# A diffusion trunk on one core: the instruction scheduler takes its times from another source

## Chip, core and metric

The kernel runs on one core of a Trainium2 chip. The metric is device time in microseconds (us). The median of three runs of the kernel before is 2285.17 us (2284.51 to 2285.52).

## What is computed

A trunk of two layers over 256 latent tokens and 256 context tokens of width 1024, all in float32. Each layer is a half-step SwiGLU feed-forward, three token mixers side by side (windowed attention, dense attention, a bidirectional mLSTM) with one output projection, and a second half-step feed-forward. Every one of these has a normalisation modulated by the conditioning vector (adaLN) ahead of it and a gated residual behind it. From the reference:

```
def modulated_norm(x, mod, k, norm_g):
    return rms_norm(x, norm_g[2 * k]) * (1 + mod[:, :, 3 * k + 1]) + mod[:, :, 3 * k]

def gated_residual(x, y, mod, k, norm_g, weight):
    return x + weight * mod[:, :, 3 * k + 2] * rms_norm(y, norm_g[2 * k + 1])

def half_ffn(x, mod, k, norm_g, w):
    h = modulated_norm(x, mod, k, norm_g)
    return gated_residual(x, swiglu(h, *w), mod, k, norm_g, FFN_RESIDUAL)
```

The output is the latent stream, so the last layer's output projection and last feed-forward work on the 256 latent tokens alone.

## The kernel before

Every float32 product is made of three matmuls over a high and a low half of each operand (`mm3`, L189 to L191):

```
mm(out, lh, rh, start=start, stop=False, **kw)
mm(out, lh, rl, start=False, stop=False, **kw)
mm(out, ll, rh, start=False, stop=stop, **kw)
```

Weights come in units of up to 128 x 1024. `dma_unit` (L148) loads a unit into one of 4 raw buffers by SP's queue; `cvt_unit` makes its high half on ScalarE (L158, tiles hi) and its low half on VectorE (L159, tiles lo), with 5 buffers of each. Activations are split in the same way by `split` (L184 on ScalarE, L185 on VectorE). The adaLN weights of the first sub-layer come in eight slices and are multiplied on TensorE (L315); those of later ones are multiplied on VectorE (L350, L352).

Ahead of a sub-layer each stream of 256 tokens is squared and summed (L440, ScalarE), brought to a reciprocal root by small steps on VectorE (L206 to L215), scaled (L445 VectorE, L447 ScalarE, one block of 128 tokens each), transposed on TensorE by 16 matmuls against the identity (L462), and taken out of PSUM with the modulation (L470 VectorE, L472 ScalarE). Behind it the closing matmuls of each 512 columns are summed (L490), squared (L555 ScalarE), multiplied by the gate (L557), summed up (L564) and added to the residual (L568, all VectorE). Latent and context streams follow each other, so that the matmuls of one cover the normalisation of the other.

Attention goes by items of a head and a block of queries: scores (L1005 to L1008), maximum (L1009, VectorE), exponential (L1023, ScalarE), scaling (L1035, GpSimd), transposes of the probabilities (L1047, TensorE) with a split, products with the values (L1062, L1064). Between items stand matmul groups of other projections as fillers.

`run_tasks` walks a list of tasks, each with the weight units that it needs, and writes conversions up to 2 units and loads up to 3 units ahead of the use. What it writes is not the final order: the Tile framework orders the instructions of each engine by a simulated list schedule over the whole program, in which an instruction's place comes from its dependences, its priority (the order of writing, less 400 for a few marked `URGENT`) and the times that the scheduler has for it. Engines then run their queues in that order. The context manager that does this is opened in `kernel`:

## Time and profile before

| | |
|---|---|
| median of 3 runs | 2285.17 us |
| the profiled execution | 2287.55 us |
| its span | 2285.8 us (1.75 us lie around it) |
| granted TensorE clock, mean | 0.987 |
| TensorE busy | 2203.2 us, 96% |
| VectorE busy | 1546.8 us, 68% |
| ScalarE busy | 984.7 us, 43% |
| GpSimd busy | 132.3 us, 6% |

The page is of one execution. Busy time of TensorE is the time in which a matmul is shown in flight. "Idle before" in a row, in square brackets, is the time in which the engine did nothing ahead of that instruction, with what ended it. [...]

### The profile page before, as it was taken

Reading aid. Unit: us, or ns where it says so; the run is one execution under the profiler, and the core shown is the slowest. Engines: PE = TensorE matmul, PEld = TensorE weight load, DVE = VectorE, ACT = ScalarE, POOL = GpSimd, SP = SyncE. Lnnn points to the kernel's source line nnn. Section 1 sums busy time; section 2 is a strip of 40 time slices with the busy share of each in tenths; the row PEclk is TensorE's granted clock in tenths of the full one; section 3 lists DMA queues with packets and bytes.
Section 4 is the critical chain, followed back from the end, with each engine's and each line's share of the span. In section 5 each row is a group of like instructions: output and inputs, shape, how many; then the busy total and the mean of one; then the engine's idle time right before and its main releaser. Section 6 shows DMA issues by size and latency. Waiting matters only on the chain.

```text
span 2285.8 us, 30617 instructions
## 1 busy us (share of the span) xinstructions
PE 2203.2 (96%) x11666; PEld 1843.7 (81%) x11666; DVE 1546.8 (68%) x2756; ACT 984.7 (43%) x1565; POOL 132.3 (6%) x100
## 2 busy tenths in 40 slices
PE   6999999998899999999999999999999989998998
PEld 4877777787678888888878788777778778997997
DVE  3987785788776654564444378778859877866556
ACT  3322223556677423442222253222226468755444
POOL 0000000023520000000000000000000241000000
PEclk9999999999999999999999999999999999998999
DMA  7665564421022223434434336665634203465554
GB/s 280 217 199 187 163 202 134 140 75 39 31 85 72 82 93 129 138 121 129 130 110 138 101 107 203 194 193 177 222 114 158 83 20 121 140 222 174 188 190 153
DMA packets 123523, 322.98 MB, mean 141 GB/s; under 512 B 12392, under 2 KB 25768, under 8 KB 122608
## 3 DMA queue, kind: packets, MB, share of 16 engines
q1 hardware_dynamic: 110224, 309.83, 41.9%
q10 hardware_dynamic: 13152, 11.21, 1.6%
q8 instruction: 91, 1.49, 0.3%
q14 instruction: 56, 0.46, 0.1%
HBM read 316.72 MB, written 4.28 MB: 140 GB/s over the span
## 4 chain that ended last, share of the span: by engine, by line
PE 86%; DVE 7%; ACT 4%; issue 1%; DMA 1%; POOL 1%; ACTq 0%; POOLq 0%; DVEq 0%
PE ps L189 27%; PE ps L190 27%; PE ps L191 26%; PE ps L1236 1%; DVE sm L1009 1%; ACT t L1023 1%; PE ps L1047 1%; PE ps L1205 1%; PE ps L360 1%; DVE lo L159 1%; PE ps L462 1%; POOL t L1035 1%; DVE slot L952 1%; ACT hi L158 1%; DVE t L185 1%
## 5 line engine op out<-in xcount | busy, mean ns | idle before, releaser
L158 ACT ACTIVATE hi<-raw 128x1024 fp32r<-128x1024 f32 (+1 forms) x444 | 457.0, 1032 | 785.8 <-PE ps L190 274.2
L189 PE MATMUL ps<-slot,hi 128*128 128x512 f32 (+1 forms) x2232 | 778.9, 351 | 6.0 <-ACT slot L184 5.2
L190 PE MATMUL ps<-slot,hi 128*128 128x512 f32 (+1 forms) x2232 | 776.2, 348 | 0.9 <-DVE slot L185 0.7
L191 PE MATMUL ps<-slot,lo 128*128 128x512 f32 (+1 forms) x2232 | 773.9, 347 | 0.0
L159 DVE TENSOR_TENSOR lo<-raw,hi 128x1024 fp32r<-128x1024 f32 (+1 forms) x444 | 525.9, 1187 | 286.8 <-ACT hi L158 285.1
L189 PEld LDWEIGHTS ps<-slot,hi 128*128 128x128 f32 x2232 | 420.1, 189 | 74.6 <-ACT slot L184 6.6
L191 PEld LDWEIGHTS ps<-slot,lo 128*128 128x128 f32 x2232 | 421.6, 189 | 57.9
L190 PEld LDWEIGHTS ps<-slot,hi 128*128 128x128 f32 x2232 | 421.8, 189 | 56.5 <-DVE slot L185 1.7
L189 PE MATMUL ps<-hi,slot 128*128 128x512 f32 (+2 forms) x1048 | 400.6, 383 | 2.3 <-ACT slot L184 1.1
L191 PE MATMUL ps<-hi,slot 128*128 128x512 f32 (+2 forms) x1048 | 398.6, 381 | 0.0
L190 PE MATMUL ps<-lo,slot 128*128 128x512 f32 (+2 forms) x1048 | 398.6, 380 | 0.0
L352 DVE SCALAR_TENSOR_TENSOR t<-raw,sc,t 128x1024 f32<-128x1024 f32 x224 | 280.2, 1280 | 130.7 <-DMA raw<-in_w_ada_dram 130.6
L1035 POOL TENSOR_SCALAR t<-t,sm 128x512 f32<-128x512 f32 (+1 forms) x96 | 132.1, 1388 | 1772.2 <-DVE sm L1032 1697.9
L189 PEld LDWEIGHTS ps<-hi,slot 128*128 128x128 f32 x1048 | 197.0, 188 | 46.7 <-issue 6.6
L191 PEld LDWEIGHTS ps<-hi,slot 128*128 128x128 f32 x1048 | 196.8, 188 | 39.7
L190 PEld LDWEIGHTS ps<-lo,slot 128*128 128x128 f32 x1048 | 197.0, 188 | 38.2
L184 ACT ACTIVATE slot<-t 128x512 fp32r<-128x512 f32 (+1 forms) x138 | 80.7, 594 | 188.1 <-DVE t L600 162.9
L600 DVE TENSOR_TENSOR t<-ps,t 128x512 f32<-128x512 f32 (+1 forms) x88 | 54.6, 620 | 86.5 <-PE ps L191 85.2
L185 DVE TENSOR_TENSOR slot<-t,slot 128x512 fp32r<-128x512 f32 (+1 forms) x138 | 87.4, 642 | 4.9 <-ACT slot L184 4.5
L1047 PE MATMUL ps<-ident,t 128*128 128x128 f32 x320 | 50.4, 289 | 24.2 <-POOL t L1035 16.4
L1047 PEld LDWEIGHTS ps<-ident,t 128*128 128x128 f32 x320 | 38.1, 146 | 35.4 <-POOL t L1035 23.0
L184 ACT ACTIVATE t<-ps 128x512 fp32r<-128x512 f32 x80 | 45.2, 596 | 48.9 <-PE ps L1047 44.9
(192 smaller groups left out, 1703.8 us busy)
## 6 DMA issues: line engine op xcount, KB each, us to landing
raw<-in_w_gu_dram SPq DMA_DIRECT2D x176, 512.0 KB
raw<-in_w_ada_dram SPq DMA_DIRECT2D x128, 512.0 KB
raw<-in_w_down_dram SPq DMA_DIRECT2D x92, 512.0 KB
raw<-in_w_fm_dram SPq DMA_DIRECT2D x64, 512.0 KB
raw<-in_w_br_dram SPq DMA_DIRECT2D x24, 512.0 KB
raw<-in_w_out_dram SPq DMA_DIRECT2D x24, 512.0 KB
slot<-in_w_ada_dram SPq DMA_DIRECT2D x16, 512.0 KB
raw<-in_w_down_dram SPq DMA_DIRECT2D x20, 256.0 KB
```

Of the source, the lines that this page charges most:

```text
L158: self.nc.scalar.activation(out=hi, in_=raw, func=AF.Copy)
L159: self.nc.vector.tensor_tensor(out=lo, in0=raw, in1=hi.bitcast(F32), op=ALU.subtract)
L184: self.nc.scalar.activation(out=hi, in_=src, func=AF.Copy)
L185: self.nc.vector.tensor_tensor(out=lo, in0=src, in1=hi.bitcast(F32), op=ALU.subtract)
L189: mm(out, lh, rh, start=start, stop=False, **kw)
L190: mm(out, lh, rl, start=False, stop=False, **kw)
L191: mm(out, ll, rh, start=False, stop=stop, **kw)
L352: v.scalar_tensor_tensor(out=acc, in0=units[0], scalar=c, in1=acc, op0=ALU.mult, op1=ALU.add)
L360: nc.tensor.matmul(ps[r:r + 32, :], self.ones.to_broadcast([P, 32]), st["acc"][s][:, j * 512:(j + 1) * 512], start=True, stop=True)
L600: nc.vector.tensor_tensor(out=hid[:, :W], in0=ps[:, :W], in1=hid[:, :W], op=ALU.mult)
L1035: nc.gpsimd.tensor_scalar(out=t[:, :nkey], in0=t[:, :nkey], scalar1=r[:, e:e + 1], scalar2=None, op0=ALU.mult)
L1047: nc.tensor.transpose(pt[:, n * P:(n + 1) * P], e[n % 2][:, kb * P:(kb + 1) * P], self.ident)
```

## The change

One argument of the context manager. The times by which the scheduler simulates the program come from a simulator of engine timelines instead of the framework's usual estimate. No task, tile size or operation is touched.

```
-    with tile.TileContext(nc) as tc:
+    with tile.TileContext(nc, schedule_with_timeline_sim=True) as tc:
```

TensorE, VectorE and GpSimd run the same instructions on the same tiles as before; GpSimd in the same order, SP's queue apart from its first 29 rows too. On TensorE some 2,250 instructions stand elsewhere, on VectorE 1,700, on ScalarE 800. ScalarE has 40 loads of an activation table instead of 49.

At the start, ScalarE's queue before, from the evacuation of the first adaLN products on (hi_26 to hi_51 are halves of weight units, slot_2 is the context, slot_38 the split latent tokens):

```order
L196 ACTIVATE t5_29_166<-ps_13_111 128x512
L158 ACTIVATE hi_26_156<-raw_12_109 128x1024
L472 ACTIVATE t5_43_199<-ps_42_194,modT_5_90,Amod_6_91 128x256
L158 ACTIVATE hi_31_179<-raw_22_139 128x1024
L472 ACTIVATE t5_45_209<-ps_44_204,modT_5_90,Amod_6_91 128x256
L158 ACTIVATE hi_47_227<-raw_25_149 128x1024
L184 ACTIVATE slot_38_190<-t5_43_199 128x2x256
L184 ACTIVATE slot_38_190<-t5_45_209 128x2x256
L440 ACTIVATE t5_56_268,sm_55_267<-slot_2_80 128x1024
L158 ACTIVATE hi_51_247<-raw_28_160 128x1024
```

The same place of ScalarE's queue now:

```order
L196 ACTIVATE t5_29_166<-ps_13_111 128x512
L158 ACTIVATE hi_47_227<-raw_25_149 128x1024
L440 ACTIVATE t5_56_268,sm_55_267<-slot_2_80 128x1024
L440 ACTIVATE t5_57_270,sm_55_267<-slot_2_80 128x1024
L472 ACTIVATE t5_43_199<-ps_42_194,modT_5_90,Amod_6_91 128x256
L472 ACTIVATE t5_45_209<-ps_44_204,modT_5_90,Amod_6_91 128x256
L158 ACTIVATE hi_51_247<-raw_28_160 128x1024
L184 ACTIVATE slot_38_190<-t5_43_199 128x2x256
L184 ACTIVATE slot_38_190<-t5_45_209 128x2x256
```

The two splits moved behind both squares of the context and behind hi_51; the conversions hi_26 and hi_31 moved ahead of this piece. On SP's queue three weight units, raw_11, raw_12 and raw_22, now stand ahead of the eight adaLN slices, where one did.

From the first feed-forward to the mixer in layer 0, ScalarE's queue before (slot_1 is the latent stream, ps_503 to ps_509 its transposes, hi_539 to hi_543 the halves of the units of the closing matmuls and of the mixer):

```order
L158 ACTIVATE hi_511_3168<-raw_490_3072 128x1024
L158 ACTIVATE hi_539_3260<-raw_495_3092 128x1024
L447 ACTIVATE t10_482_3013<-slot_1_79,sm_479_2998 128x1024
L472 ACTIVATE t5_504_3121<-ps_503_3116,modT_5_90,Amod_6_91 128x256
L472 ACTIVATE t5_506_3131<-ps_505_3126,modT_5_90,Amod_6_91 128x256
L184 ACTIVATE slot_499_3112<-t5_504_3121 128x2x256
```

And now:

```order
L158 ACTIVATE hi_511_3168<-raw_490_3072 128x1024
L158 ACTIVATE hi_539_3260<-raw_495_3092 128x1024
L158 ACTIVATE hi_541_3264<-raw_498_3110 128x1024
L447 ACTIVATE t10_482_3013<-slot_1_79,sm_479_2998 128x1024
L158 ACTIVATE hi_543_3268<-raw_513_3172 128x544
L555 ACTIVATE t5_514_3182,pss_485_3061<-slot_185_1229 128x512
L555 ACTIVATE t5_515_3184,pss_485_3061<-slot_185_1229 128x512
L472 ACTIVATE t5_504_3121<-ps_503_3116,modT_5_90,Amod_6_91 128x256
```

A conversion, hi_541, moved ahead of L447, and a second one with the two squares of the closing ahead of the evacuations; on TensorE the 16 transposes moved behind the last 12 closing matmuls. The other three entries of a two-stream sub-layer read alike, with one or two conversions ahead of L447.

From the mixer to the last feed-forward in layer 1, VectorE's queue before (slot_3000 is the latent stream, ps_3041 and ps_3047 the last closing sums, pss_3042 their squares):

```order
L557 TENSOR_TENSOR slot_3016_17558<-ps_3047_17677,slot_2999_17502 128x512
L211 SCALAR_TENSOR_TENSOR sm_3039_17631<-sm_3038_17630,sm_3037_17629 128x1
L564 TENSOR_TENSOR sm_3055_17717<-pss_3042_17667 128x1
L159 TENSOR_TENSOR lo_3090_17835<-raw_3053_17706,hi_3089_17834 128x1024
L215 SCALAR_TENSOR_TENSOR sm_3038_17630<-sm_3039_17631,sm_3038_17630 128x1
L206 TENSOR_SCALAR sm_3056_17719<-sm_3055_17717 128x1
L159 TENSOR_TENSOR lo_3094_17869<-raw_3081_17799,hi_3093_17868 128x1024
```

And now:

```order
L159 TENSOR_TENSOR lo_3090_17835<-raw_3053_17706,hi_3089_17834 128x1024
L568 SCALAR_TENSOR_TENSOR slot_3000_17504<-slot_3016_17558,sm_3033_17615,slot_3000_17504 128x1024
L159 TENSOR_TENSOR lo_3094_17869<-raw_3081_17799,hi_3093_17868 128x1024
L206 TENSOR_SCALAR sm_3037_17629<-sm_3035_17626 128x1
L207 TENSOR_SCALAR sm_3038_17630<-sm_3037_17629 128x1
L211 SCALAR_TENSOR_TENSOR sm_3039_17631<-sm_3038_17630,sm_3037_17629 128x1
L557 TENSOR_TENSOR slot_3016_17558<-ps_3041_17642,slot_2999_17502 128x512
L215 SCALAR_TENSOR_TENSOR sm_3038_17630<-sm_3039_17631,sm_3038_17630 128x1
L557 TENSOR_TENSOR slot_3016_17558<-ps_3047_17677,slot_2999_17502 128x512
L564 TENSOR_TENSOR sm_3055_17717<-pss_3042_17667 128x1
```

Both low halves, and the first block's L568, moved ahead of the last two L557; on ScalarE the four conversions hi_3077 to hi_3093 moved ahead of the last L440 and both L555 in the same way.

In the two attentions the filler matmuls moved ahead among the items: in layer 0 the query projections of the dense attention (four groups) and later the mLSTM's, in layer 1 one set. On VectorE some low halves and the logarithms of the mLSTM gates (L1099 to L1110) moved ahead of the key and query columns. In the very last stage three closing groups of matmuls are interleaved.

## Rows read from the trace of the kernel before

**Rows 1.** Busy us, share of the span and instructions of each engine.

```profile
PE 2203.2 (96%) x11666; PEld 1843.7 (81%) x11666; DVE 1546.8 (68%) x2756; ACT 984.7 (43%) x1565; POOL 132.3 (6%) x100
```

**Rows 2.** The chain that ended last, by engine.

```profile
PE 86%; DVE 7%; ACT 4%; issue 1%; DMA 1%; POOL 1%; ACTq 0%; POOLq 0%; DVEq 0%
```

**Rows 3.** Stretch, us; busy PE, PEld, DVE, ACT, POOL; clock; DMA share; GB/s.

```profile
0.00:57.00 57.00, 39.20 (x229) 24.45 (x229) 22.00 (x73) 21.07 (x32) 0.19 (x4) 0.94 0.77 281
...
457.00:690.00 233.00, 209.77 (x1187) 175.35 (x1186) 186.18 (x473) 150.74 (x316) 81.16 (x64) 0.96 0.18 58
690.00:1314.00 624.00, 623.38 (x2932) 514.12 (x2931) 320.32 (x603) 227.93 (x326) 0.00 (x0) 1.00 0.35 113
...
1786.00:1930.00 144.00, 127.87 (x765) 109.10 (x764) 111.46 (x252) 95.19 (x181) 50.97 (x32) 0.94 0.20 63
...
2057.00:2115.00 58.00, 47.29 (x297) 42.64 (x296) 39.98 (x75) 31.10 (x47) 0.00 (x0) 0.88 0.53 174
...
2257.00:2286.00 29.00, 19.75 (x86) 15.62 (x84) 19.59 (x38) 10.72 (x17) 0.00 (x0) 0.91 0.32 110
```

**Rows 4.** Timeline of TensorE at the start: start, duration, instruction, idle before.

```profile
27.42 0.62 PE L189 MATMUL ps<-slot,hi 128*128 128x256 f32 x3 [4.27 <-ACT slot L184]
28.76 0.58 PE L190 MATMUL ps<-slot,hi 128*128 128x256 f32 x1 [0.72 <-DVE slot L185]
...
52.82 0.66 PE L391 MATMUL ps<-ident,t 128*128 128x128 f32 x4 [0.81 <-DVE t L198]
```

**Rows 5.** Timeline of ScalarE at the start.

```profile
23.57 0.56 ACT L472 ACTIVATE t<-ps,modT,Amod 128x256 f32<-128x256 f32 x1 [0.50 <-DVE t L470]
...
26.75 1.14 ACT L184 ACTIVATE slot<-t 128x512 fp32r<-128x512 f32 x2
28.25 1.06 ACT L440 ACTIVATE t<-slot 128x1024 bf16<-128x1024 f32 x1 [0.36 <-DMA slot<-in_ctx_dram]
29.21 0.19 ACT L440 ACTIVATION_READ_ACCUMULATOR t<-slot 128x1 f32 x1
```

**Rows 6.** Timeline of ScalarE where the mixer of layer 0 is entered.

```profile
412.58 1.06 ACT L158 ACTIVATE hi<-raw 128x1024 fp32r<-128x1024 f32 x1 [0.51 <-ACT t L555]
415.38 1.06 ACT L158 ACTIVATE hi<-raw 128x1024 fp32r<-128x1024 f32 x1 [1.74 <-PE ps L191]
416.35 1.13 ACT L447 ACTIVATE t<-slot,sm 128x1024 f32<-128x1024 f32 x1
```

**Rows 7.** Timeline of TensorE at the second stream of the four entries.

```profile
435.59 1.94 PE L462 MATMUL ps<-ident,t 128*128 128x128 f32 x16 [1.57 <-DVE t L445]
...
990.61 0.66 PE L462 MATMUL ps<-ident,t 128*128 128x128 f32 x4 [0.24 <-ACT t L472]
...
1364.46 1.81 PE L462 MATMUL ps<-ident,t 128*128 128x128 f32 x12 [0.34 <-DVE t L445]
...
1756.25 0.63 PE L462 MATMUL ps<-ident,t 128*128 128x128 f32 x4 [1.25 <-DVE t L445]
```

**Rows 8.** Timeline of VectorE and TensorE from mixer to feed-forward in layer 1.

```profile
2077.40 1.23 DVE L159 TENSOR_TENSOR lo<-raw,hi 128x1024 fp32r<-128x1024 f32 x1 [0.48 <-ACT hi L158]
...
2081.07 1.12 PE L462 MATMUL ps<-ident,t 128*128 128x128 f32 x4 [5.85 <-DVE t L445]
2082.01 1.28 DVE L568 SCALAR_TENSOR_TENSOR slot<-slot,sm,slot 128x1024 f32<-128x1024 f32 x1
...
2087.04 2.82 PE L462 MATMUL ps<-ident,t 128*128 128x128 f32 x12 [4.86 <-DVE t L445]
```

**Rows 9.** TensorE's waits, 457 to 690: us in total, times, longest.

```profile
PE ps L1047 <- POOL t L1035: 10.7, 12, 2.3
PE ps L1062 <- DVE t L185: 6.1, 3, 4.5
```

**Rows 10.** Two short stretches, columns as in rows 3: the granted clock.

```profile
434.00:440.00 6.00, 3.33 (x23) 2.77 (x23) 4.25 (x11) 4.57 (x9) 0.00 (x0) 1.00 0.11 44
581.00:591.00 10.00, 7.91 (x26) 6.33 (x27) 4.21 (x9) 4.42 (x9) 3.46 (x3) 0.50 0.12 41
```

## Prediction

> **What bounds the kernel now.** I read the busy times first, then the chain that ended last, then TensorE's busy time stage by stage, and only then single waits. TensorE is busy 2203.2 of 2285.8 us [rows 1] and its matmuls are 86% of the chain [rows 2], so a new order of the same instructions can gain at most the 82.6 us in which it is idle, and little of that is free. The stages show where it lies [rows 3]: 17.8 us in the first 57, 23.2 in the layer-0 attention (457 to 690), 16.1 in the layer-1 attention (1786 to 1930), 10.7 where layer 1 goes from mixer to last feed-forward (2057 to 2115), 9.3 at the end. In the 624 us from 690 to 1314 it is idle 0.6 us. Two thirds of the kernel is therefore full, and can only lose. In the two attentions VectorE is the next engine, 186 of 233 us and 111 of 144, so idle time there isn't simply a matter of order either.
>
> The changed build holds the same tiles and tasks on TensorE, VectorE and GpSimd. ScalarE has nine fewer table loads (16 to 11 at L1218, 16 to 12 at L1312, 5 to 4 at L1023, one more at L1103). They stand almost only in the mLSTM and merge stages, inside the stretch without idle time, so I cost them at nothing: TensorE's own matmuls hide them there.
>
> **The start.** Before, TensorE's first matmul of a feed-forward comes at 27.42, after a wait of 4.27 for the split on ScalarE [rows 4]. In the new order the two splits stand behind both squares of the context stream (L440), two evacuations (L472) and the conversion hi_51. The context arrives for ScalarE at 28.25 [rows 5]. It can't come sooner: in both orders twelve 512-KB transfers are ahead of it on SP's queue, and the DMA engines carry 281 GB/s over this stage [rows 3]. So: 28.25, two L440 of 1.06 with their reads of 0.19 to 30.75, two L472 of 0.56 to 31.9, hi_51 of 1.06 to 32.9 and a first split of about 0.6 [rows 5, 6], which is 33.5 and 6 us later than before. The other move is that three weight units now pass the eight slices of the first adaLN weights on SP's queue; the last slice becomes the eleventh transfer rather than the ninth, about 3 us later. The first evacuation then moves from 23.57 to about 26.5, still ahead of 30.75, so this one is hidden by the wait for the context. What comes back: all five units are converted when the matmuls start, and the three small waits at the stage's end, of which the largest is 0.81 [rows 4], can vanish, 1.6 us together. I take **+5**; the bounds are +3 (the 0.72 at 28.76 goes as well and the smaller steps overlap) and +9 (VectorE, which now also has two adaLN products put early, gives the low half late).
>
> **Four entries with two streams** (about 416, 960, 1345 and 1728). Before, the latent stream's normalised tokens are transposed (16 matmuls, L462) among the last closing matmuls of the sub-layer that ends, so that the first matmul of the next one follows without a wait. In the new order all 16 stand behind the closing matmuls, and ScalarE has a conversion (hi_541 at the first) ahead of the normalisation L447 which feeds them. That conversion waits for a buffer which TensorE must give back: the two conversions before it start at 412.58 and 415.38, the second after a wait for TensorE [rows 6], so one buffer comes free each 2.8 us, the next at 418.2. The conversion then ends at 419.2, and L447, at 416.35 before, starts there: 2.85 us late, and with it the transposes, the evacuations behind them and the next sub-layer's first matmul. TensorE has only the closing matmuls meanwhile, which it had before too, so the 2.8 appear as a wait. Queued behind the waiting ScalarE are L447 and, on VectorE, the L470 evacuations; TensorE waits for those. A part comes back at the second stream, whose chain sets a wait of its own: 1.57 us at 435.59, 0.24 and a like piece at 991 (0.6 together), 0.34 and two like it at 1364 to 1368 (0.9), 1.25 at 1756 [rows 7]. A late TensorE finds these ready. Four times 2.8 less 4.3 is **+6.9**. Bounds: 0 if the buffers come free one unit sooner, since the closing matmuls now run without transposes between them; +11 if nothing comes back.
>
> **Mixer to feed-forward in layer 1** (2060 to 2090). One stream is left, so nothing covers the chain of the last normalisation: TensorE waits 5.85 and 4.86 us. Before, ScalarE squares the two closing halves between the conversions, and VectorE's residual step for the last block (L568) starts at 2082.01 with two low-half conversions, 1.23 us each, in its chain [rows 8]. Now four conversions on ScalarE come ahead of the squares, and both low halves and the first block's L568 ahead of VectorE's L557. The last conversion ended at 2078.6 before (2077.58 + 1.06); issued a unit earlier it ends at about 2077.4. Behind it L440 and two L555 take 2.3 us, L557 and the eight small steps 3.7 to 4.5, so the last L568 starts at 2083.4 to 2084.2 rather than 2082.01. The first block's transposes are late too, but wait for nothing else. **+2.5**, bounds 0 and +5.
>
> **The two attentions.** The projections that fill TensorE's gaps while softmax waits (23 us of query projections and 45 us of mLSTM projections in layer 0, 17 us in layer 1, by the count of their matmuls at the traced step) are moved ahead by up to 8, 12 and 11 us of work and run out sooner, at the first probability transposes rather than item by item. The waits there are mostly for GpSimd's scaling (10.7 us in 12 waits) and for VectorE's low halves (6.1 us in 3) [rows 9]. If each gap that loses its filler becomes a wait, this costs 31 us; but TensorE is not the only limit, and work done ahead shortens the gaps later, as the 4.54 at 520.42 stands just where layer 0 runs out of its first set. At best half of the 39 us now idle comes back, a gain of 20. Between these ends I choose **+4.5** for both: nearest to the sum of those gaps of 0.5 to 2.3 us which are at present covered two or three times by a filler, less the big one.
>
> **The end.** The last sub-layer's closing groups are interleaved rather than one after the other; the last 21 matmuls and the chain behind are as before. **+0.5** (0 to +1.5).
>
> Sum: 5 + 6.9 + 2.5 + 4.5 + 0.5 = **+19.4 us** on the profiled execution's 2287.55, so 2306.9; that run is 2.4 above the median of the three, so **2304.5**.
>
> **The rivals.**
> *Clock.* [...] Chance 0.14.
>
> *Packing in the attentions outweighs all else.* There the low halves, the key and query columns and the gate logarithms get new places on VectorE. If TensorE's fillers being early lets scores and transposes of the following items be issued as soon as VectorE and GpSimd are free, half of the 39 us comes back. Against the 14.9 us of the other terms that gives -5, and with the entries at their lower bound -12: 2273 to 2280. It decides if more than 19 us come back. For it speaks that waits for GpSimd dominate and GpSimd is busy only 81 of 233 us [rows 3]; against it, its order is unchanged and VectorE is 80% busy. Chance 0.13.
>
> *Nothing measurable.* The entries are absorbed (buffers come free sooner, 0), the attentions give 5 back, and start and 2080 s cost +5: 2281 to 2289. Chance 0.13, also for a build whose moves all fall into waits that stay.
>
> *All covers lost.* Start, entries and 2080 as forecast and the full 31 us in the attentions: 2330. Chance 0.06.
>
> **How the numbers follow.** My forecast, 2290 to 2315, has 0.54. The range takes in the clock rival and stops above the faster one: 2282 to 2322; about 0.13 lies below and 0.07 above. 0.2% is 4.6 us, about what a measurement of this kernel tells from no change. Slower: 0.54 + 0.14 + 0.06 = 0.74; same 0.13; faster 0.13.
>
> **What would show it.** First feed-forward matmul at 33 rather than 27.4. Before the first matmul after each of the four entries a wait of 2 to 3 us, and a smaller one for the second stream. L447 at the first entry about 2.8 us after its conversion's neighbour. The second wait around 2087 grown by 2 to 3. Idle time in the attentions within 5 us of 23 and 16. If 690 to 1314 shows idle time beyond the entry at 960, I have missed a stage; if the attentions' idle time falls by 19, the second rival is right; if the granted clock falls at the entries, the first.

## The result and the profile after

The changed kernel takes 2355.56 us (median of 4 runs, 2353.65 to 2357.57) against 2285.35 for the kernel before beside it: a ratio of 1.0306, interval 1.0294 to 1.0319. That is 70 us slower, where 19 were forecast. The profiled execution took 2356.38 us, its span is 2354.6, its mean granted clock 0.976.

From the page after: TensorE's and its neighbours' busy time, which answers to [rows 1], the chain's shares by engine, which answer to [rows 2], and the group of the first of the three products (line, engine, shapes, count; busy us, mean ns; idle before).

```profile
PE 2225.7 (95%) x11666; PEld 1864.1 (79%) x11666; DVE 1551.1 (66%) x2756; ACT 971.1 (41%) x1556; POOL 130.8 (6%) x100
...
PE 85%; DVE 7%; ACT 3%; DMA 3%; issue 2%; POOL 0%; ACTq 0%; DVEq 0%; POOLq 0%
...
L189 PE MATMUL ps<-slot,hi 128*128 128x512 f32 (+1 forms) x2232 | 779.2, 352 | 11.7 <-ACT slot L184 11.5
```

The same 11666 matmuls are busy 22.5 us longer, and the idle time is 128.9 us (2354.6 less 2225.7) where it was 82.6: 46.3 more. The two make up the span's 68.8. The longer busy time is put down to the clock: all but 1.0 us of it lies in stretches whose granted clock is lower than before, 10.9 us of it in the layer-0 attention, at 0.93 against 0.96.

To place them, each stretch of before was matched with the stretch after in which the same matmuls run (to within two of them). TensorE's windows after: stretch, us, busy (matmuls), clock, DMA share, GB/s.

```profile
0.00:104.79 104.79, 82.03 (x470) 0.95 0.70 247
...
274.68:331.13 56.45, 52.70 (x222) 0.94 0.61 183
...
411.02:477.17 66.15, 60.51 (x311) 0.95 0.38 121
477.17:742.64 265.47, 227.67 (x1220) 0.93 0.18 56
742.64:992.70 250.06, 250.06 (x1160) 1.00 0.30 100
...
1056.78:1377.36 320.58, 320.58 (x1397) 1.00 0.40 124
1377.36:1433.44 56.08, 50.11 (x333) 0.97 0.28 86
...
1765.77:1821.30 55.53, 51.85 (x269) 1.00 0.48 153
1821.30:2000.75 179.45, 156.14 (x962) 0.93 0.22 71
...
2106.90:2179.00 72.10, 58.65 (x381) 0.88 0.58 192
```

The same stretches of before lasted 100, 50, 60, 240, 250, 320, 50, 53, 170 and 70 us. The first entry, the first attention, the last entry and the second attention before:

```profile
400.00:460.00 60.00, 57.33 (x311) 1.00 0.41 133
460.00:700.00 240.00, 216.77 (x1220) 0.96 0.19 62
...
1712.00:1765.00 53.00, 51.75 (x267) 1.00 0.50 157
1765.00:1935.00 170.00, 153.87 (x964) 0.95 0.22 70
```

The differences, in us:

| stage | forecast | measured | of it busy (clock) | of it idle |
|---|---|---|---|---|
| start | +5 | +4.8 | -0.1 | +4.9 |
| before 331 (adaLN of the next sub-layer) | 0 | +6.5 | +2.7 | +3.8 |
| four two-stream entries | +6.9 | +18.8 | +6.8 | +12.1 |
| two attentions | +4.5 | +34.9 | +13.2 | +21.8 |
| mixer to feed-forward, layer 1 | +2.5 | +2.1 | -0.6 | +2.7 |
| the end | +0.5 | -0.2 | | |
| all else | 0 | +1.9 | | |

Three terms came out within 0.7 us. The entries cost nearly three times, the attentions nearly eight times their term, and one stage was not in the sum.

### The profile page after: what moved, and what is told of

Read it like the earlier page. It is cut to its first block, busy times and chain, and to the rows that moved or that the text cites. A ratio compares the mean times of both kernels' runs of the same rounds, so it can differ in the third digit from the quotient of the medians.

```text
span 2354.6 us, 30663 instructions
## 1 busy us (share of the span) xinstructions
PE 2225.7 (95%) x11666; PEld 1864.1 (79%) x11666; DVE 1551.1 (66%) x2756; ACT 971.1 (41%) x1556; POOL 130.8 (6%) x100
## 4 chain that ended last, share of the span: by engine, by line
PE 85%; DVE 7%; ACT 3%; DMA 3%; issue 2%; POOL 0%; ACTq 0%; DVEq 0%; POOLq 0%
PE ps L189 26%; PE ps L190 26%; PE ps L191 26%; PE ps L1236 1%; DMA raw<-in_w_ada_dram 1%; DVE lo L159 1%; DVE sm L1009 1%; ACT t L1023 1%; DVE t L185 1%; DVE t L352 1%; PE ps L1205 1%; PE ps L360 1%; PE ps L1047 1%; DMA slot<-in_w_ada_dram 1%; PE ps L1062 1%
## 5 line engine op out<-in xcount | busy, mean ns | idle before, releaser
L189 PE MATMUL ps<-slot,hi 128*128 128x512 f32 (+1 forms) x2232 | 779.2, 352 | 11.7 <-ACT slot L184 11.5
L191 PE MATMUL ps<-slot,lo 128*128 128x512 f32 (+1 forms) x2232 | 777.8, 349 | 0.0
L159 DVE TENSOR_TENSOR lo<-raw,hi 128x1024 fp32r<-128x1024 f32 (+1 forms) x444 | 527.8, 1190 | 311.5 <-ACT hi L158 308.3
L189 PEld LDWEIGHTS ps<-slot,hi 128*128 128x128 f32 x2232 | 422.8, 191 | 79.6 <-ACT slot L184 15.0
L191 PEld LDWEIGHTS ps<-slot,lo 128*128 128x128 f32 x2232 | 425.0, 190 | 57.3
L189 PE MATMUL ps<-hi,slot 128*128 128x512 f32 (+2 forms) x1048 | 401.6, 384 | 7.8 <-ACT slot L184 7.8
L191 PE MATMUL ps<-hi,slot 128*128 128x512 f32 (+2 forms) x1048 | 397.8, 382 | 0.0
L352 DVE SCALAR_TENSOR_TENSOR t<-raw,sc,t 128x1024 f32<-128x1024 f32 x224 | 278.9, 1281 | 153.9 <-DMA raw<-in_w_ada_dram 153.6
L189 PEld LDWEIGHTS ps<-hi,slot 128*128 128x128 f32 x1048 | 198.7, 190 | 53.2 <-ACT slot L184 8.5
L191 PEld LDWEIGHTS ps<-hi,slot 128*128 128x128 f32 x1048 | 198.2, 190 | 40.0
L1062 PE MATMUL ps<-t,slot 128*128 128x256 f32 x160 | 48.7, 323 | 22.4 <-DVE t L185 10.9
L1009 DVE TENSOR_REDUCE sm<-ps 128x1 f32<-128x512 f32 (+1 forms) x96 | 53.5, 591 | 14.0 <-PE ps L1008 13.7
```

The source lines that it names most:

```text
L159: self.nc.vector.tensor_tensor(out=lo, in0=raw, in1=hi.bitcast(F32), op=ALU.subtract)
L352: v.scalar_tensor_tensor(out=acc, in0=units[0], scalar=c, in1=acc, op0=ALU.mult, op1=ALU.add)
L1009: v.tensor_reduce(out=mx[:, e:e + 1], in_=ps[:, :nkey], axis=AX.X, op=ALU.max)
L1062: nc.tensor.matmul(o, V, hi[:, kb].rearrange("p h q -> p (h q)"), start=(kb == 0), stop=(kb == nkb - 1), skip_group_check=True)
```

## The experiments

**How they are made.** A kernel that keeps part of the old order builds the program twice, reads each engine's order from both, and builds it again with every queue tied to a chosen order by added dependences:

```
+    for stream in pin(traced):
+        for p, q in zip(stream, stream[1:]):
+            tc.add_manual_dep(traced[q], traced[p].name, mybir.DependencyInfo(
+                mybir.DependencyClass.NoSync, mybir.DependencyReason.DATA), reason="pin")
```

`KEEP` gives stretches of a queue that keep the old order, `MOVES` single instructions put behind another. All compute the whole trunk. Ratios are to the kernel before beside each run; over the study its medians were 2285.4 to 2289.0.

| run | us | ratio, interval |
|---|---|---|
| e1_l447_first | 2356.42 | 1.0313, 1.0297 to 1.0328 |
| e2_ada_behind | 2350.21 | 1.0283, 1.0266 to 1.0300 |
| e3_keys_first | 2349.60 | 1.0282, 1.0267 to 1.0297 |
| e4_attn_vec_old | 2373.70 | 1.0385, 1.0369 to 1.0400 |
| f0_new_order | 2352.43 | 1.0287, 1.0271 to 1.0303 |
| f1_attn_first_third | 2340.03 | 1.0237, 1.0217 to 1.0257 |
| f2_attn_second_third | 2339.98 | 1.0236, 1.0218 to 1.0255 |
| f3_attn_last_third | 2351.04 | 1.0283, 1.0266 to 1.0299 |
| g1_entries_old | 2334.52 | 1.0199, 1.0184 to 1.0215 |
| g2_entries_vec_old | 2367.36 | 1.0342, 1.0325 to 1.0359 |
| g3_attn1_old | 2336.94 | 1.0212, 1.0198 to 1.0226 |
| g4_old_gate_rows_later | 2289.96 | 1.0004, 0.9996 to 1.0013 |
| h1_entry_pattern_new | 2305.58 | 1.0075, 1.0058 to 1.0091 |
| h2_entry_products_old | 2359.20 | 1.0314, 1.0298 to 1.0330 |
| h3_two_vec_moves | 2288.84 | 1.0008, 0.9999 to 1.0017 |
| i1_old_order_new_deal | 2294.26 | 1.0031, 1.0019 to 1.0042 |
| i2_new_order_old_deal | 2348.88 | 1.0267, 1.0250 to 1.0283 |
| i3_two_vec_moves_old_deal | 2281.30 | 0.9974, 0.9965 to 0.9983 |

### My reason for the entries

```
+    MOVES = {'Activation': [([2642], 2450), ([8979], 8807), ([11468], 11263)]}
```

At three entries the conversion that the new order has ahead of L447 goes behind it.

> The new order, with one move on ScalarE's queue at three of the four entries (first feed-forward to mixer and second to first feed-forward in both layers; the fourth, at 960, keeps the new order): the conversion that stands ahead of the normalisation L447 is put right behind it. These three cost 14.8 us of the 70 (6.2, 6.1 and 2.5, by the traces of before and after). Theory of the prediction, that L447 waits behind the conversion and everything follows from that: most of it comes back, 2341 to 2346 us. Rival, that the evacuations of the transposes (L470, L472) stand behind the closing sums and behind further conversions anyway, so that an early L447 only waits further on: at most 3 us come back, 2352 to 2356 us.

The rival held: no gain. Two rows of ScalarE's timeline after show the conversion and L447 (start, us, instruction, idle before).

```profile
429.15 1.06 ACT L158 ACTIVATE hi<-raw 128x1024 fp32r<-128x1024 f32 x1 [1.71 <-PE ps L191]
430.12 1.13 ACT L447 ACTIVATE t<-slot,sm 128x1024 f32<-128x1024 f32 x1
```

With 11.02 us of delay by then, L447 stands at 419.1 of before's time, 2.75 later than before [rows 6], close to the forecast's 2.85. In e1 the conversion is out of the way:

```profile
422.56 1.23 DVE L159 TENSOR_TENSOR lo<-raw,hi 128x1024 fp32r<-128x1024 f32 x1 [1.05 <-ACT hi L158]
...
424.67 1.15 ACT L447 ACTIVATE t<-slot,sm 128x1024 f32<-128x1024 f32 x1 [2.15 <-DVE sm L215]
...
431.80 0.79 PE L189 MATMUL ps<-hi,slot 128*128 128x512 f32 x1 [3.54 <-ACT slot L184]
```

L447 now waits 2.15 for VectorE's L215, and TensorE's wait before its first product is 3.54 where it was 2.88. The conversion had stood in a wait that was there anyway. Ahead of that L215 VectorE has a low half (L159), which itself waits 1.05 for its high half; that this is what makes L215 late is read from the rows and not tested by a run.

### A wait that is not the order's

```
+    MOVES = {'DVE': [([1847, 1848], 1692)]}
```

Two adaLN products (L352) near 290 us go behind the four closing sums L490 that TensorE waits for.

> The new order, with one move on VectorE's queue near 290 us: the two adaLN products of one weight unit (L352), which wait for that unit's transfer, are put behind the four closing sums (L490) which free TensorE's PSUM. Theory, that an instruction waiting for a transfer holds up ready ones behind it: the 6.45 us which this stretch lost (3.75 of waiting and 2.7 at half the clock behind it) come back, 2348 to 2350 us. Rival, that the transfer itself is late and TensorE would wait for its weights instead: 0 to 2 us, 2353 to 2356 us.

It came out at 2350.2, but in the traces of e1, e3 and e4, which don't touch this place, 0.80 us of the wait was left at most. So the changed kernel was run again, as it is:

> The changed kernel as it is, beside the runs of the same call. Theory A, that the wait of 3.75 us at L360 near 298 us hangs on when two weight transfers land and not on the order alone: it is small here as in three of the four runs before, and the time is 2349 to 2352. Theory B, that the two square steps L352 ahead of four closing steps cost 6 us in every run: 2355 to 2357, as measured first, and the 6 us of the kernel with these two moved behind were its edit's.

Theory A held, at the upper edge of its range: 2352.4. VectorE and TensorE in the profile after, then in f0:

```profile
295.56 2.48 DVE L352 SCALAR_TENSOR_TENSOR t<-raw,sc,t 128x1024 f32<-128x1024 f32 x2 [2.65 <-DMA raw<-in_w_ada_dram]
...
298.69 1.94 PE L360 MATMUL ps<-t,ones 128*32 128x512 f32 x8 [3.75 <-DVE slot L490]
```

```profile
291.53 2.48 DVE L352 SCALAR_TENSOR_TENSOR t<-raw,sc,t 128x1024 f32<-128x1024 f32 x2 [2.27 <-DMA raw<-in_w_ada_dram]
...
295.18 1.06 PE L360 MATMUL ps<-t,ones 128*32 128x512 f32 x8
```

In f0 the second weight unit landed 4 us sooner and L360 ran without a wait. Of the 14 traces of a new order here, two have the long wait (3.75, and 3.99 in i2), the others 1.41 at most. It takes the new order, which has L490 behind a product that waits for a transfer, and a transfer that lands late; e2's edit was not what gained in its run. The comparisons below are with f0.

### The layer-0 attention

Four runs on what of the new order costs there, e3 and e4 first:

```
+    MOVES = {'DVE': [([3222, 3023, 3032, 3033, 3041, 3050, 3051], 2954), ([3397, 3169, 3170,
...
+                      3191], 3075)], 'Activation': [([11436, 3171], 3106)]}   # e3: behind the key and query steps
+    KEEP = {'DVE': [(449, 943)], 'Activation': [(245, 507)]}                  # e4
```

> The new order, with moves on VectorE's queue where the layer-0 attention begins: the low half lo_657 and the evacuations of the values go behind the rotation of the keys (L741), and the low half lo_703 and the logarithms of the mLSTM gates (L1099 to L1118) go behind the key and query columns (L779, L821); on ScalarE the logarithm L1103 with its table load goes behind the query columns. TensorE's fillers stay early. The layer-0 attention cost 25.5 us of the 70. Theory that VectorE's order is the cause: 8 to 20 us come back, 2335 to 2348 us. Theory of the prediction, that TensorE's fillers being moved ahead is the cause: at most 3 us come back, 2352 to 2356 us, since the scores still stand behind the fillers.

> The new order, but between 460 and 700 us of the kernel before VectorE and ScalarE keep the order of the kernel before; TensorE keeps the new one, fillers ahead. Theory that VectorE's and ScalarE's order is the cause of the 25.5 us: 20 to 25 come back, 2331 to 2336 us. Theory that TensorE's fillers ahead are the cause: 0 to 8 come back, 2348 to 2356 us. In between, both have a share and this is its size.

e3 lies between its two ranges, and e4 above both of its own. In e3 the waits at the key transposes (L815), 2.06 and 2.44 us after, became one of 0.46, and behind them the run had gained 5.6 us on the changed kernel's profile; 40 us later all but half a microsecond of that was gone. It went right behind the last products of the query projection, in waits at the probability transposes and the next scores and in slower products behind them (0.79 us for the score product L1005 below, 0.45 on the mean before):

```profile
512.15 0.30 PE L1047 MATMUL ps<-ident,t 128*128 128x128 f32 x1 [1.45 <-issue]
...
515.45 0.79 PE L1005 MATMUL ps<-slot,slot 128*128 128x512 f32 x1 [1.69 <-ACT t L1023]
```

In e4 VectorE and ScalarE run the old order and TensorE the new: 0.0098 of the time, 22 us, over f0, and the stretch is 21 us longer in its trace. So beside TensorE's new order the new vector orders save time; what they would cost beside its old order isn't shown. Then the whole order, third by third:

```
+    KEEP = {'PE': [(2047, 2360)], 'DVE': [(449, 602)], 'Activation': [(245, 304)], 'SP': [(166, 189)]}   # f1
+    KEEP = {'PE': [(2360, 2660)], 'DVE': [(602, 746)], 'Activation': [(304, 374)]}                       # f2
+    KEEP = {'PE': [(2660, 3266)], 'DVE': [(746, 952)], 'Activation': [(374, 516)]}                       # f3
```

> New order, but in the first third of the layer-0 attention (460 to 522 us of before, key and query steps and the first score products) TensorE, VectorE, ScalarE and SyncE keep the order of before. Theory local: a stretch loses by its own order; the lag of the changed kernel grows there from 17.1 to 26.5 us, so this gains 9, with 2340 to 2348. Theory passed on: as with the key steps put first (5.6 us gained by 500 us, gone by 540), what is gained is waited for in the next third, and this gains under 3.

> New order, but in the second third of the layer-0 attention (522 to 576 us of before: score products of the middle heads, value transposes, gate of the memory branch) all engines keep the order of before. Theory local: the lag grows there from 26.5 to 40, so this gains 13, with 2335 to 2344. Theory passed on: the gain is under 4, as the first third has already delayed VectorE and what it feeds.

> New order, but in the last third of the layer-0 attention (576 to 709 us of before) all engines keep the order of before. Theory local: the lag moves there from 40 to 42.6 us (with 47 between), so this gains 3, with 2347 to 2354. Theory passed on: most of the 25 us of this attention is only paid here, where fewer filler products are left, and this gains 8 or more.

Local, for all three: they give back 0.0050, 0.0051 and 0.0004, which is 11.4, 11.7 and 0.9 us of 2286, each within 2.5 us of what its delay in the trace said, and in sum 24 of the 25.5 that the windows show. (By the intervals, a difference of two ratios here is uncertain by 5 to 6 us.) TensorE at the key transposes in f0, and the ten microseconds around them; then the matching ten in f1:

```profile
484.14 0.30 PE L815 MATMUL ps<-ident,t 128*128 128x128 f32 x1 [2.06 <-DVE t L741]
486.88 0.48 PE L815 MATMUL ps<-ident,t 128*128 128x128 f32 x1 [2.44 <-DVE t L741]
```

```profile
485.00:495.00 10.00, 8.12 (x38) 0.69 0.16 54
```

```profile
482.00:492.00 10.00, 9.16 (x41) 1.00 0.16 54
```

4.5 us of waiting, and then a granted clock of 0.69 over 485 to 495, for the products behind. These two waits are VectorE's: in both orders TensorE has 72 products of the value projection right ahead of the key transposes, and e3 shortens the waits by VectorE's order alone. What TensorE's own order changes here stands behind them. The 96 products of the query projection stood among the items in twelve pieces, the longest of 33, and now run as 3, 60, 27 and 6. That it is these fillers, rather than the order of the items themselves, which cost the rest is argued from this listing and from e3; no run moves the fillers alone, and the other half-order, TensorE old with the new vector orders, was not run.

### The entries and the layer-1 attention

```
+    KEEP = {'PE': [(1737, 2047), (4301, 4698), (6076, 6437), (7852, 8076)],                # g1 only
+            'SP': [(150, 166), (232, 246), (320, 333), (448, 464)],                        # g1 only
+            'DVE': [(347, 449), (1287, 1378), (1531, 1627), (1886, 1989)],                 # g1 and g2
+            'Activation': [(199, 245), (651, 699), (807, 853), (998, 1045)]}               # g1 and g2
+    KEEP = {'PE': [(8076, 9821)], 'DVE': [(1989, 2533)], 'Activation': [(1040, 1314)],
+            'SP': [(464, 517)]}                                                            # g3
```

> New order, but at the four two-stream entries (400 to 460, 950 to 1012, 1330 to 1385 and 1712 to 1760 us of before) all engines keep the order of before. Theory local: the entries cost what the windows of the changed kernel show, 6.2 + 4.1 + 6.1 + 2.5 = 19 us, so this gives 2332 to 2336 where the unchanged new order gave 2352.4. Theory mixed: the windows hold pieces of the neighbouring stretches and the second stream gives some of it back, as the prediction had it with 6.9, so 2343 to 2348.

> New order, but at the same four entries VectorE and ScalarE alone keep the order of before, and TensorE the new one. If the order of the evacuations and conversions is what costs there, this gains as much as all engines together, 2332 to 2340. If TensorE's place for transposes and closing products is what costs, this gains nothing or loses, 2352 to 2365, as it did in the layer-0 attention (2373.7 there).

> New order, but from the layer-1 attention to the end of the mixer behind it (1760 to 2040 us of before) all engines keep the order of before. Theory local: 9.5 us of the attention and 1.2 behind it come back, 2340 to 2343. Theory passed on: under 4 us come back, over 2348.

The entries are local: 0.0088 under f0, 20 us. With the vector orders alone back, the time rises by 0.0055, 13 us, above both ranges: the pattern of e4 again. The layer-1 attention gave back 0.0075, 17 us, more than the 10.6 that were expected from the profile after; in its trace 12.5 us of it lie in the attention, and the rest is tied to no place. The profile of before understates this stage: i1 (below), which has the same order there, passes 1765 to 1935 in 4.1 us less, 3.6 of them busy time.

What in TensorE's order costs at an entry? Its queue at the first one, in short (L462 are the transposes; products are the last twelve of the closing of the feed-forward, L189 to L191):

```
before:  4 L462 | 2 products | 12 L462 | 10 products | products of the mixer
after:   12 products | 16 L462 | products of the mixer
```

h1 puts, on the old order, TensorE's products in these new places; h2 keeps the places new and gives the products among themselves the old order.

```
+    done = iter([next(turn[x in prod]) for x in places])   # places: new in both; turn: the old order of each kind
```

> The order of before on all engines, but at the four entries TensorE's products (L189 to L191) and transposes stand in the new order's places: closing products of the first stage ahead of the sixteen transposes instead of between them; the order within each kind stays old. If this place is what costs at the entries, TensorE comes to the products of the second stage with nothing left to cover the split, and the kernel is 15 to 35 us over before (2300 to 2325). If the order within the products costs (which bank is closed first), under 4 us over before.

> The complement: the new order on all engines, but at the four entries the products among themselves keep the order of before, and only their places among the transposes are new. If the places cost, this is within 4 us of the changed kernel, a ratio of 1.027 to 1.032. If the order within the products costs, it gains 10 to 19 us, 1.020 to 1.025.

Before reading h1, i1 has to be taken off it (below): the same build with no edit is at 1.0031, so the places alone cost 0.0044, 10 us with an uncertainty of 5, and not the 17 that the ratio to before suggests; in its trace the four entries are 9.2 us longer than in i1's. h2 gains nothing, so beside the new vector orders the order within the products is not it. The trace of h1 shows the mechanism: TensorE's first product of the mixer waits, where i1 has no wait at all in this place (its first wait is the second stream's).

```profile
428.06 0.50 PE L189 MATMUL ps<-hi,slot 128*128 128x512 f32 x1 [1.23 <-ACT slot L184]
443.35 1.94 PE L462 MATMUL ps<-ident,t 128*128 128x128 f32 x16 [2.18 <-DVE t L445]
```

In the changed kernel the same places read:

```profile
431.21 1.97 PE L462 MATMUL ps<-ident,t 128*128 128x128 f32 x16 [0.75 <-DVE t L445]
436.05 0.50 PE L189 MATMUL ps<-hi,slot 128*128 128x512 f32 x1 [2.88 <-ACT slot L184]
454.19 0.61 PE L189 MATMUL ps<-hi,slot 128*128 128x512 f32 x1 [2.01 <-ACT slot L184]
```

So the place is shown for about half of the entries' 20 us. The other half comes with the order within the products and the vector orders together, which is what the new order has at the entries beyond h1. It can't be had back by halves: with the vector orders alone put back (g2) the four entries take 34 us more than before in the trace, with the products' order alone (h2) 26, in f0 20.6.

### Transfers that are dealt anew

The runs g4, h1 and h3, made on the old order, started about 6 us late in their traces, though nothing is edited there. The queues of before and i1 hold the same instructions in the same order. What differs is which of eight semaphores (DMAHW0 to 7) each transfer gets. In the listings of the two built programs they are dealt round in the order of the transfers across the engines, and that order differs, though each queue's own is the same; at the start a transfer's row names the semaphore of an earlier one, for which it waits. Two rows of ScalarE's queue in the two listings:

```
before:  L263 DMA gqk [waits DMAHW4]   L263 DMA nsink [waits DMAHW5]
i1:      L263 DMA gqk [waits DMAHW1]   L263 DMA nsink [waits DMAHW3]
```

i1 is the old order with the new dealing, i2 the new order with the old scheduler's dealing:

```
+    queues = build(False)[1]                                # i1: the order of before
+    nc, _ = build(True, lambda traced: queues.values())     #     scheduled with the timeline simulator
+    queues = build(True)[1]                                 # i2: the new order
+    nc, _ = build(False, lambda traced: queues.values())    #     scheduled without it
```

> Every engine's order is that of before; the new scheduler only deals the transfers to the eight transfer semaphores (DMAHW0 to 7), and with them decides for which earlier transfer each issue waits. If the dealing matters, TensorE's first product of the first stage stands near 34 us instead of 27, as in the three runs made in this way on the old order, and the time is 2288 to 2293. If those starts were the runs' own, this is 2285 to 2287, ratio 0.999 to 1.001.

> Every engine's order is that of the changed kernel; the transfers are dealt by the scheduler of before. If the start's 4.8 us come from the dealing, the first product stands near 28 and this is 3 to 6 us under the changed kernel, ratio 1.026 to 1.028. If they come from the order (ScalarE's splits behind the context squares, as the prediction had it), the first product stays near 32 and the ratio is 1.028 to 1.031.

The dealing alone costs 0.0031, 7 us, on the old order. ScalarE in i1 (ACTq is its queue issuing a transfer), and TensorE's first product:

```profile
12.00 0.34 ACTq L263 DMA_DIRECT2D gqk<-in_gqk_dram  x1
...
15.81 0.33 ACTq L263 DMA_DIRECT2D nsink<-in_sink_dram  x1
...
20.81 1.15 ACT L447 ACTIVATE t<-slot,sm 128x1024 f32<-128x1024 f32 x1 [7.21 <-DMA raw<-in_w_gu_dram]
...
27.64 0.60 ACT L196 ACTIVATE t<-ps 128x512 f32<-128x512 f32 x1 [5.68 <-issue]
...
34.36 1.01 PE L189 MATMUL ps<-slot,hi 128*128 128x256 f32 x3 [3.24 <-ACT slot L184]
```

Parameter transfers stand on ScalarE's queue ahead of its work. In i1 nsink goes out 3.8 us behind gqk, where before it was 0.4 (10.54 and 10.96), and the engine's work waits behind the issues: L447 stands 7.21 us, put down to a transfer of weights that it doesn't read, and L196 is followed back to the issues alone. The first product starts at 34.36 instead of 27.42 [rows 4]. In the new order the dealing hardly counts at the start: in i2 the first product stands at 33.09, in f0 at 32.48. There the late start is the order's, as the prediction said. i2's ratio, 1.0267, lies in the range of the first expectation and just under f0's interval, but the start is not where it gains: by the windows it is 6.4 us longer than before in i2 and 5.1 in f0. Its four runs fall into two pairs, near 2351.4 and 2346.1; the traced one, of the upper pair, has the long wait near 300 us. Against f0 its trace gains 3.0 us at the entry near 1785, all of it busy time of the matmuls, in a stretch with a granted clock of 0.94 in f0, and 3.5 in the attention behind.

### A faster kernel

```
+    MOVES = {'DVE': [([3343, 3344, 3345, 3346, 3347, 3349, 3348, 3350, 3351, 3352, 3353, 3354, 3355,
+                       3356, 3357, 3358], 3387),                                # g4 only: gate rows at 520
+                     ([12059, 12060, 12061, 12062, 12063, 12065, 12064, 12066, 12067, 12068, 12069, 12070,
+                       12071, 12072, 12073, 12074], 12103),                     # g4, h3, i3: the same at 1820
+                     ([14513, 14514, 14515, 14516], 14587), ([14662], 14597),
+                     ([14692], 14629)]}                                         # g4, h3, i3: 2077 to 2087
```

> The order of before everywhere, with only VectorE edited: the short steps of the memory gate's row (L1135 to L1146) stand behind the scaling L185 that TensorE waits 4.54 us for at 520 us (and likewise in layer 1), and at 2077 to 2087 us three splits stand behind the steps that TensorE waits for. If a wait on VectorE in these places is on the path that sets the end, 2275 to 2281: 2 to 6 at 520, 2 at 1820, 3 at 2080. If the next thing TensorE needs is late as well (as when the key steps were put first), 2283 to 2286.

> The order of before with two of the three moves on VectorE of the run with the gate rows later: the gate's row behind the scaling at 1820 us, and three splits behind the steps that TensorE waits for at 2077 to 2087 us. In that run's trace these two gained 5.3 and 3.5 us; the third, at 520 us, only moved the wait of 4.5 us to the next transposes (5.0 us) and is left out. If what the trace shows is time, 2 to 9 us under before, ratio 0.996 to 0.999; if the changes of that trace were its run's own, 0.9995 to 1.001.

> The order of before with the same two moves on VectorE as in the run of two moves, now with the transfers dealt as before. If the 6 us that its start lost to the dealing hid the gain, this is 2277 to 2283, ratio 0.996 to 0.999. If the two waits come back elsewhere, 0.9995 to 1.001.

g4 came out above both of its ranges, at 2290.0. Its first move takes the wait at 520 us away and gets it back at the next transposes; before, then g4:

```profile
520.42 0.58 PE L1062 MATMUL ps<-t,slot 128*128 128x256 f32 x1 [4.54 <-DVE t L185]
```

```profile
532.15 1.11 PE L1047 MATMUL ps<-ident,t 128*128 128x128 f32 x4 [5.04 <-DVE t L185]
```

The moves at 2077 to 2087 gain: the second wait of 4.86 [rows 8] is 1.27 in i3.

```profile
2081.33 1.12 PE L462 MATMUL ps<-ident,t 128*128 128x128 f32 x4 [6.16 <-DVE t L445]
2083.71 2.82 PE L462 MATMUL ps<-ident,t 128*128 128x128 f32 x12 [1.27 <-DVE t L445]
```

h3 has the new scheduler's dealing, i3 that of the old, and in h3 the dealing hid the gain. The four runs agree: edits without dealing 0.9974, edits with it 1.0008, dealing without edits 1.0031, so the edits give 0.0023 to 0.0026 and the dealing takes 0.0031 to 0.0034. i3, 2281.3 us, is faster than the kernel before by 6 us, and so than both kernels. Of the 5.3 us that its trace gains near 1820, 3.1 also show in i1, which has no edit there, so most of that is not the edit's; the wait of 2.2 us at 1820, which is gone in i3, is.

## Why the prediction was right and wrong

The direction was right, for reasons that held in part; the time lies 34 us above the range.

**The start**, +5: right, in size and reason. The order and not the dealing is the cause (i2), and the first product follows the context's first square by 4.6 us in each of three traces: 26.87 and 31.48 in the profile after, 27.86 and 32.48 in f0, 28.48 and 33.09 in i2. It came at 31.48 rather than 33.5, in the main because the context landed 1.4 us sooner than before [rows 5], which the prediction had ruled out. ScalarE and TensorE after:

```profile
26.87 1.06 ACT L440 ACTIVATE t<-slot 128x1024 bf16<-128x1024 f32 x1 [1.47 <-DMA slot<-in_ctx_dram]
...
30.80 1.14 ACT L184 ACTIVATE slot<-t 128x512 fp32r<-128x512 f32 x2
```

```profile
31.48 1.44 PE L189 MATMUL ps<-slot,hi 128*128 128x256 f32 x5 [5.44 <-ACT slot L184]
```

**The entries**, +6.9: the wait was right in size, its cause and its sum were not. TensorE's first product waits 2.88, 2.92 and 2.93 us at three of the entries, as forecast with 2.8. But the conversion ahead of L447 isn't the cause (e1); I followed one chain into L447 and didn't look which other input would be late with it. The step "a part comes back at the second stream", -4.3, failed too: the second stream waits 2.01 at 454.19, and over the four entries its waits add up to 5.2 us where they were 5.4; only at 1756 did they come back whole. And slow products came behind the waits, 6.8 us in sum, at a granted clock of 0.95, 0.97, 0.97 and 1.00 over the four stretches where all had 1.00 before. I had named the transposes' new place and costed it at nothing, "TensorE has only the closing matmuls meanwhile, which it had before too": their place behind the transposes had been what covered the evacuations (h1, 10 us).

**The attentions**, +4.5: this is the step that broke the forecast. The term's mechanism, fillers that run out sooner, is the one that the rows speak for, and its upper bound was 31 us, "if each gap that loses its filler becomes a wait". Measured were 35 by the windows, 41 by the runs; the idle time, which was to stay within 5 us of 23 and 16, came to 38 and 23. Two things were missing: the products ran at a lower granted clock, 0.93 in both attentions after against 0.96 and 0.95 before, which is 13.2 of the 34.9, and the gaps that appear are not only the old ones, since key steps on VectorE became late as well. That it is the fillers that cost the rest is not shown apart from TensorE's other moves. I took a value near the middle because "TensorE is not the only limit"; the rows gave no reason for that. e4 and g2 show how far off, for the two halves of the order set against each other: with the vector orders unchanged, TensorE's new order costs 46 us in the layer-0 attention (24 + 22) and 33 at the entries (20 + 13).

**Mixer to feed-forward, the end, table loads, the full stretch**: +2.1 for +2.5 (its own steps give 1.4 to 2.2, less than was taken), -0.2 for +0.5, and no idle time between 743 and 993 or 1057 and 1377. "Can only lose" held for the stretch at 290 us, in some executions.

**The clock rival**, that products behind each of the four new waits run at a lower granted clock, was right that the clock falls, but had neither the price nor the place. Its price was an estimate from [rows 10]: half of the 7.91 us that are busy there at 0.50, so 4 us at each entry, 16 in all, and 2320, which the range takes in. No run shows this price at the entries: they brought 6.8, from 0.1 to 3.2 each, and the attentions, which it left out, 13.2 of the 22.5. At the entry near 1790 a wait of 2.93 left the granted clock at 1.00 over the stretch in the profile after; the same order, with the same wait, in f0:

```profile
1790.06 0.50 PE L189 MATMUL ps<-hi,slot 128*128 128x512 f32 x1 [2.93 <-ACT slot L184]
1790.40 0.39 PE L190 MATMUL ps<-lo,slot 128*128 128x512 f32 x1
```

```profile
1782.07 0.80 PE L189 MATMUL ps<-hi,slot 128*128 128x512 f32 x1 [2.93 <-ACT slot L184]
1782.67 0.63 PE L190 MATMUL ps<-lo,slot 128*128 128x512 f32 x1
```

There the granted clock is 0.94 over the stretch and its matmuls are busy 3.0 us longer than before, where after it was 1.00 and 0.1. In nine traces that have the entries' new order unedited, the three waits of 2.88 to 2.93 us are the same to 0.01 us, and the stretch's matmuls are busy between 0.0 and 3.2 us longer, 1.3 on the mean. At 485 to 495 f0 has 0.69 behind two waits of 4.5 us together. Why one wait of 2.93 is followed by 0.94 and another by 1.00 is not shown by any run.

**What I had not seen** is the dealing of transfers, 7 us on the old order. It stands in the waits of the two builds' transfers; I had compared their order alone.

## What to carry to other kernels

A filler matmul was worth here the wait that it stood in, plus what the matmuls behind that wait lost at a lower granted clock, 0 to 3.2 us behind one and the same wait of 2.9; so forecast it as a range. An order that runs fillers in a row may spend them, so cost each gap that loses one as a wait until a row says otherwise. When two engines' orders change together, restore a whole stretch on all engines to size it, and one engine alone only to learn how far the orders are fitted to each other: put back alone (e4, g2), a part cost more than it saved. Before a build with the same order is called the same program, compare what its transfers wait for.

## What was not expected of the hardware and the tools around it

- The order of issue is the same in the kernel before and in i1; 7 us lie in which earlier transfer each transfer waits for.
- One program loses 6.5 us in one execution and none in another at the same place, by a weight transfer that lands 4 us later (295.56 against 291.53).
- One and the same wait, 2.93 us near 1790 us of the same order, left the granted clock at 1.00 over its stretch in one execution and at 0.94 in another (f0); behind waits of 2.06 and 2.44 within 3 us it was 0.69 over 485 to 495 (f0).
